# Expert stage of a diffusion-trunk kernel: one stream of 1 MB weight halves in a fixed order on three engines

## Chip, cores and metric

The kernel runs on one core of a Trainium2 chip. The metric is the device time of one launch in microseconds. The kernel before takes 2043.71 us (median of 3 runs, 2041.2 to 2043.97).

## What is computed

One layer of a trunk over 1024 latent tokens of width 1024 with a context prefix of 256: a token mixer, then an expert-choice SwiGLU mixture of 16 experts, then a final RMSNorm. The change concerns the mixture. Each expert takes the 128 tokens with the highest affinity for it:

```python
def expert_choice_ffn(h, w_router, w_gate, w_up, w_down):
    cap = EC_CAPACITY * n // N_EXPERTS                      # 128
    aff = softmax(h @ w_router, axis=-1)
    g, idx = lax.top_k(swapaxes(aff, 1, 2), cap)
    xg = h[bidx, idx]
    hid = silu(xg @ w_gate[e]) * (xg @ w_up[e])             # D_FF = 2816
    y = (hid @ w_down[e]) * g[..., None]
    return zeros_like(h).at[bidx, idx].add(y)
```

All is float32. The 16 experts have 16 x 3 x 1024 x 2816 weights, 554 MB, and each is read once.

## The kernel before

The mixer (the prologue) takes the first 435 us; the change leaves it alone. The rest, `moe`, is the expert stage.

Tiles. The hidden width 2816 of an expert is cut into six pieces j: five of 512 columns and one of 256. For each piece there is a gate-and-up unit and a down unit. A gate block or an up block of a 512 piece is 2 MB (128 partitions x 4096 words); the gate and up blocks of the 256 piece share one 2 MB array (`wt`); a down block is 2 MB, the last one 1 MB (`wdt`). An expert thus has 33 halves of 1 MB (128 x 2048 words), loaded in 17 transfers.

Splitting. TensorE (PE) is fed with a product of three: each float32 operand is split into a high and a low part (`split`, lines 226 to 232). ScalarE (ACT) copies the half to `hi` (line 227), VectorE (DVE) subtracts to get `lo` (line 228). `mm3` (line 611) issues hi*hi, hi*lo, lo*hi, so a half of 2048 columns costs 12 matmuls of 512 columns, in the 256 piece 24 of 256. There are five `raw` buffers of 2 MB (`NRAW`) and four `hi`/`lo` pairs of one half each (`NHL`): the pair of half m is free for half m+4 once the matmuls of half m are done.

Loop. For each expert e and piece j: `gate_up` (loads, splits, 48 matmuls to PSUM tile `gu`, Silu on ACT at line 1567, product on DVE at 1568, four transposes on PE to `ht` at 1572, split to `hh` and `hl`), then `down` of the piece before (24 matmuls to `y`). Behind the last piece of an expert, `y` is scaled on DVE (1597) and scatter-added to DRAM by GpSimd (POOL, 1598).

Beside it: a search for each expert's threshold (15 rounds `topk_iter`, two after each unit from n=1 to n=8: two DVE operations, eight PE matmuls to `tc`, four DVE operations; then `topk_end`, on DVE and POOL). Experts 0 and 1 have their tokens ranked in the prologue; expert 2 is the first that needs the search. `prep(e+1)` builds a one-hot matrix `oh` on DVE, gets the token numbers (`px`, `idx`) and gates (`pg`) by matmuls, and starts the gather `xg` on POOL (1451); `prep_t(e+1)` transposes and splits the rows to `xgh` and `xgl`. `last` (1621 to 1669) is the final norm.

Order. A scheduler lays out each engine's stream: it takes the program's order as priority and moves instructions past each other by its own account of when they will be ready. A few instructions are pinned by hand (`pin`), and `issue_after` puts the side work behind one split. Each engine works its stream off in that order.

## Time and profile before

| | us |
|---|---|
| median of 3 runs | 2043.71 |
| the profiled execution's own time | 2039.89 |
| its span, first to last instruction | 2038.0 |
| PE busy | 1911.7 (94%) |
| DVE busy | 1740.3 (85%) |
| ACT busy | 1334.7 (65%) |
| POOL busy | 203.4 (10%) |
| HBM read | 622.98 MB |

Times are microseconds from the span's start. A busy PE is not PE at its peak: matmuls overlap, and one of 512 columns is recorded with 0.39 us while the next starts 0.227 us after it. So the starts are read here, not the busy share. "[1.35 <-DVE lo L228]" says that the engine was idle for 1.35 us ahead of the instruction and that the `lo` of line 228 on DVE ended that. The granted TensorE clock is 0.976 on average; 1.00 stands for 2.4 GHz and 0.50 for 1.2 GHz.

### The profile page before, as it was taken

What the parts mean: (1) busy time and instruction counts of PE and PEld (TensorE: products, weight loads), DVE (VectorE), ACT (ScalarE), POOL (GpSimd) and SP (SyncE); (2) the same over time, 40 slices, a digit from 0 to 9 for tenths busy, and PEclk for the clock granted to TensorE, in tenths of its full rate; (3) what the DMA queues carried; (4) which work ended last, traced back from release to release, by engine and by line L of the source; (5) the groups of instructions that cost most, each with busy time, mean ns of one, the idle gap of its engine ahead of it and who ended that gap; (6) DMA issues with size and microseconds to landing.
All of it is one profiled execution on the core that took longest, in us unless ns stands there. A gap on an engine that the chain in (4) does not pass through costs nothing.

```text
span 2038.0 us, 23678 instructions
## 1 busy us (share of the span) xinstructions
PE 1911.7 (94%) x9434; PEld 1554.7 (76%) x9434; DVE 1740.3 (85%) x1641; ACT 1334.7 (65%) x1104; POOL 203.4 (10%) x141
## 2 busy tenths in 40 slices
PE   7989989959998999999999999999999999999994
PEld 2777778848887878787878787878787878778774
DVE  7888887799997888888888888888888898888886
ACT  6568643356775767676776676767667677676675
POOL 2311101130002000000010101010101010100011
PEclk9999989969999999999999999999999999999997
DMA  8444553579897989898999989898989898989994
GB/s 321 125 139 143 193 191 131 219 273 364 328 379 303 369 331 394 335 397 339 392 343 363 376 355 382 350 388 344 386 346 389 347 381 352 384 337 391 347 380 175
DMA packets 77517, 651.26 MB, mean 320 GB/s; under 512 B 8695, under 2 KB 16424, under 8 KB 42206
## 3 DMA queue, kind: packets, MB, share of 16 engines
q1 hardware_dynamic: 64286, 602.54, 75.5%
q0 software_dynamic: 10816, 38.82, 6.5%
q10 hardware_dynamic: 2304, 8.39, 1.0%
q8 instruction: 74, 1.21, 0.2%
q14 instruction: 37, 0.30, 0.0%
HBM read 622.98 MB, written 26.74 MB: 319 GB/s over the span
## 4 chain that ended last, share of the span: by engine, by line
PE 73%; DVE 12%; DMA 6%; issue 5%; ACT 3%; POOL 1%; SPq 0%; POOLq 0%; DVEq 0%; ACTq 0%
PE gu L611 43%; PE y L611 21%; DVE lo L228 5%; DMA mraw<-in_wmod_dram 3%; PE mx L611 3%; ACT hi L227 2%; PE ht L1572 2%; DVE macc L839 1%; DMA wm<-in_wmod_dram 1%; DVE ys L1597 1%; DMA trr<-in_trig_dram 1%; PE pq L611 1%; DVE g L716 1%; DMA x<-in_x_dram 1%; DMA accx<-xr 1%
## 5 line engine op out<-in xcount | busy, mean ns | idle before, releaser
L228 DVE TENSOR_TENSOR lo<-raw,hi 128x2048 fp32r<-128x2048 f32 (+1 forms) x531 | 1183.1, 2270 | 114.4 <-ACT hi L227 112.5
L227 ACT ACTIVATE hi<-raw 128x2048 fp32r<-128x2048 f32 (+1 forms) x531 | 981.2, 1894 | 85.1 <-PE gu L611 72.1
L611 PE MATMUL gu<-lo,xgh 128*128 128x512 f32 (+1 forms) x1536 | 579.7, 377 | 34.5 <-DVE lo L228 34.5
L611 PE MATMUL gu<-hi,xgh 128*128 128x512 f32 (+1 forms) x1536 | 575.7, 375 | 1.8 <-ACT xgh L227 1.6
L611 PE MATMUL gu<-hi,xgl 128*128 128x512 f32 (+1 forms) x1536 | 573.4, 373 | 1.7 <-DVE xgl L228 1.7
L611 PEld LDWEIGHTS gu<-lo,xgh 128*128 128x128 f32 x1536 | 290.1, 189 | 98.4 <-DVE lo L228 49.9
L611 PEld LDWEIGHTS gu<-hi,xgh 128*128 128x128 f32 x1536 | 290.2, 189 | 53.4 <-ACT xgh L227 2.1
L611 PEld LDWEIGHTS gu<-hi,xgl 128*128 128x128 f32 x1536 | 290.2, 189 | 51.6 <-DVE xgl L228 2.9
L611 PE MATMUL y<-hi,hl 128*128 128x512 f32 x704 | 280.6, 399 | 0.0
L611 PE MATMUL y<-lo,hh 128*128 128x512 f32 x704 | 279.0, 396 | 0.0
L611 PE MATMUL y<-hi,hh 128*128 128x512 f32 x704 | 275.7, 392 | 0.0
L1567 ACT ACTIVATE hid<-gu 128x512 f32<-128x512 f32 x96 | 54.0, 563 | 296.2 <-PE gu L611 296.2
L1598 POOL DMA_INDIRECT accx<-ys,idx x15 | 50.7, 3379 | 1125.6 <-DVE ys L1597 1051.0
L611 PEld LDWEIGHTS y<-lo,hh 128*128 128x128 f32 x704 | 132.6, 188 | 26.6
L611 PEld LDWEIGHTS y<-hi,hh 128*128 128x128 f32 x704 | 132.8, 189 | 25.5
L611 PEld LDWEIGHTS y<-hi,hl 128*128 128x128 f32 x704 | 132.9, 189 | 24.7
L227 ACT ACTIVATE hh<-ht 128x512 fp32r<-128x512 f32 x96 | 53.8, 561 | 88.9 <-PE ht L1572 88.9
L1568 DVE TENSOR_TENSOR hid<-hid,gu 128x512 f32<-128x512 f32 x96 | 61.5, 640 | 50.5 <-ACT hid L1567 49.4
L228 DVE TENSOR_TENSOR hl<-ht,hh 128x512 fp32r<-128x512 f32 x96 | 61.4, 640 | 4.3 <-ACT hh L227 4.3
L1451 POOL DMA_INDIRECT xg<-hxd,idx x16 | 42.3, 2642 | 210.6 <-DVE idx L1440 161.0
L1572 PE MATMUL ht<-k_ident,hid 128*128 128x128 f32 x352 | 54.7, 274 | 2.0 <-DVE hid L1568 2.0
L839 DVE SCALAR_TENSOR_TENSOR macc<-mraw,cond,macc 128x512 f32<-128x512 f32 x56 | 41.8, 748 | 16.1 <-DMA mraw<-in_wmod_dram 15.3
(425 smaller groups left out, 1862.4 us busy)
## 6 DMA issues: line engine op xcount, KB each, us to landing
raw<-in_wg_dram SPq DMA_DIRECT2D x80, 2048.0 KB, 9.8
raw<-in_wu_dram SPq DMA_DIRECT2D x80, 2048.0 KB, 10.6
raw<-in_wd_dram SPq DMA_DIRECT2D x78, 2048.0 KB, 9.7
raw<-in_wt_dram SPq DMA_DIRECT2D x15, 2048.0 KB, 10.0
mraw<-in_wmod_dram POOLq DMA_DIRECT2D x32, 512.0 KB, 4.6
raw<-in_wdt_dram SPq DMA_DIRECT2D x16, 1024.0 KB, 7.9
wm<-in_wmod_dram SPq DMA_DIRECT2D x16, 512.0 KB, 9.8
wr<-in_win_dram SPq DMA_DIRECT2D x24, 256.0 KB, 3.5
```

Source lines behind the costliest of these rows:

```text
L227: i = self.nc.scalar.activation(hi, src, AF.Copy)
L228: j = (eng or self.nc.vector).tensor_tensor(lo, src, hi, op=ALU.subtract)
L611: i = nc.tensor.matmul(out, l, r, start=st, stop=sp)
L716: V.tensor_tensor_scan(g[:, s], a[:, s], r[:, s], 0.0, op0=ALU.mult, op1=ALU.add)
L839: nc.vector.scalar_tensor_tensor(acc, w[:, i], c, acc, op0=ALU.mult, op1=ALU.add)
L1451: nc.gpsimd.indirect_dma_start(out=xg, out_offset=None, in_=self.hxd, in_offset=bass.IndirectOffsetOnAxis(ap=idx[:, :1], axis=0))
L1567: nc.scalar.activation(hid[:, 0:w], p[:, 0, 0:w], AF.Silu)
L1568: nc.vector.tensor_tensor(hid[:, 0:w], hid[:, 0:w], p[:, 1, 0:w], op=ALU.mult)
L1572: nc.tensor.transpose(q[:, 128 * b:128 * b + 128], hid[:, 128 * b:128 * b + 128], self.ident)
L1597: nc.vector.scalar_tensor_tensor(ys, self.y, gate, self.g2b, op0=ALU.mult, op1=ALU.mult)
L1598: nc.gpsimd.indirect_dma_start(out=self.accx, out_offset=bass.IndirectOffsetOnAxis(ap=idx[:, :1], axis=0), in_=ys, in_offset=None, compute ...
```

## The change

The weights of the stage become one list `S` of 528 halves (33 per expert) in the order in which PE uses them. Every half is loaded by itself (10 `raw` buffers of 1 MB instead of five of 2 MB), split by itself and multiplied by itself. The loop runs over the list: matmuls of half m, Silu and product where it ends a unit, split of half m+4 (`cut`), load of half m+10, then what `plan` has put behind half m. PE, ACT and DVE work in exactly the order of the program (`manual_schedule`); POOL and the queue of loads (SP) are still laid out by the scheduler. The transposes of `hid` follow one half after the end of their unit. The search takes one round every three halves, with the comparison (`topk_a`) three halves ahead of its matmuls (`topk_p`). `px` and `pg` become one PSUM tile, issued together. The one-hot matrix of the next expert is built four halves after the start of its host's second unit (fourth for expert 1) and multiplied two halves after the start of the next unit; the gathered rows are transposed in the fifth unit (sixth for expert 1). The finer cutting of the last two units (`DL`, `DS`, `FROM`) goes. Numbers of halves, buffers of `hi`/`lo`, matmuls and bytes stay.

```diff
--- before.py
+++ after.py
-    def topk_iter(self, i):
+    def topk_a(self, i):
+        V = self.nc.vector
+        cand, ge = self.tk[:2]
...
+    def topk_p(self, i):
+        ge = self.tk[1]
+        self.pc = self.pt(f"tc{i}")[:, 0:3 * E]
         for b in range(8):
-            nc.tensor.matmul(pc, self.ones2, ge[:, b].rearrange("p e q -> p (e q)"), start=b == 0, stop=b == 7)
-        V.tensor_scalar(g3.rearrange("p e q -> p (e q)"), pc, CAP - 0.5, None, op0=ALU.is_ge)
+            self.nc.tensor.matmul(self.pc, self.ones2, ge[:, b].rearrange("p e q -> p (e q)"), start=b == 0, stop=b == 7)
+
+    def topk_b(self, i):
+        V, T = self.nc.vector, self.T
+        g3, s3, inc = self.tk[2:]
...
-    NRAW, NHL = 5, 4
-    DL, DS, FROM = 2048, 1024, 95
+    NRAW, NHL = 10, 4
...
+    def gather(self, e, idx):
+        xg = self.mo.tile([128, D], F32, tag="xg", name=f"xg{e}", bufs=1)
+        self.nc.gpsimd.indirect_dma_start(out=xg, out_offset=None, in_=self.hxd,
+                                          in_offset=bass.IndirectOffsetOnAxis(ap=idx[:, :1], axis=0))
+        self.xe[e] = xg, idx
     def prep(self, e):
...
+        oh = self.mo.tile([128, 8, 128], BF16, tag="oh", name=f"oh{e}", bufs=1)
+        idx = self.mo.tile([128, 1], I32, tag="idx", name=f"idx{e}", bufs=3)
         g = self.mo.tile([128, 1], F32, tag="gate", name=f"gate{e}", bufs=3)
-        self.gate_pick(self.pt(f"pg{e}"), self.oh, self.aux[:, :, e], g)
+        slot = self.slot[:, e] if e < NR else self.slT[:, :, e]
+        self.nc.vector.tensor_tensor(oh, self.iota[:, None, :].to_broadcast([128, 8, 128]),
+                                     slot[:, :, None].to_broadcast([128, 8, 128]), op=ALU.is_equal)
+        yield
+        p = self.pt(f"px{e}")
+        for b in range(8):
+            self.nc.tensor.matmul(p[:, 0:2], oh[:, b], self.tokb[:, b], start=b == 0, stop=b == 7)
+        for b in range(8):
+            self.nc.tensor.matmul(p[:, 2:5], oh[:, b], self.aux[:, b, e], start=b == 0, stop=b == 7)
+        with self.nc.allow_low_precision(reason="whole numbers below 2**24"):
+            self.nc.vector.tensor_reduce(idx, p[:, 0:2], axis=mybir.AxisListType.X, op=ALU.add)
+        self.nc.vector.tensor_reduce(g, p[:, 2:5], axis=mybir.AxisListType.X, op=ALU.add)
+        self.gather(e, idx)
...
+    def make_stream(self):
+        a = self.a
+        self.S, self.at, self.end = [], {}, {}
+
+        def gu(e, j):
+            self.at[e, j] = len(self.S)
+            if j < 5:
+                for g, n in ((0, "wg"), (1, "wu")):
+                    for h in range(2):
+                        self.S.append(("g", e, j, g, h, a[n][e, j][:, 2048 * h:2048 * h + 2048]))
+            else:
+                for g in range(2):
+                    self.S.append(("g", e, j, g, 0, a["wt"][e][:, 2048 * g:2048 * g + 2048]))
+            self.end[e, j] = len(self.S) - 1
+
+        def dn(e, j):
+            if j < 5:
+                for h in range(2):
+                    self.S.append(("d", e, j, 0, h, a["wd"][e, j][:, 2048 * h:2048 * h + 2048]))
+            else:
+                self.S.append(("d", e, j, 0, 0, a["wdt"][e]))
+
+        prev = None
+        for e in range(E):
+            for j in range(6):
+                gu(e, j)
+                if prev is not None:
+                    dn(*prev)
+                prev = e, j
+        dn(*prev)
...
+        self.raws, self.hls = {}, {}
+        for m in range(2):
+            self.hls[m] = self.hl_tile(m)
+        for m in range(8):
+            self.load(m)
+        for m in range(8, 10):
+            self.raws[m] = self.raw_tile(f"raw{m}")
+        self.n0 = 0
...
-        t = self.ma.tile([128, 4096], F32, tag=f"raw{self.nr % self.NRAW}", name=name, bufs=1)
+        t = self.ma.tile([128, 2048], F32, tag=f"raw{self.nr % self.NRAW}", name=name, bufs=1)
...
-    def unit_tiles(self, w):
...
-    def load_unit(self, src, w=4096, fine=False):
...
-    def gate_up(self, e, j):
...
+    def load(self, m):
+        M = len(self.S)
+        if m < M:
+            self.raws[m] = self.raw_tile(f"raw{m}")
+            self.nc.sync.dma_start(self.raws[m], self.S[m][5])
+        elif m < M + 4:
+            t = 2 * (m - M)
+            src = self.accx.rearrange("(t p) c -> p t c", p=128)
+            self.fin.append(self.raw_tile(f"fin{t}"))
+            self.nc.sync.dma_start(self.fin[-1].rearrange("p (t c) -> p t c", t=2), src[:, t:t + 2])
+
+    def cut(self, m, pin=False):
+        if m >= len(self.S):
+            return
+        self.hls[m] = self.hl_tile(m)
+        self.split(self.raws.pop(m), *self.hls[m], pin=pin)
+
+    def half(self, m):
+        _, e, j, g, h, _ = self.S[m]
+        hi, lo = self.hls.pop(m)
+        if self.S[m][0] == "g":
+            xh, xl = self.xe[e][:2]
+            if g + h == 0:
+                self.gu[e, j] = self.pm.tile([128, 2, 512], F32, tag="gu", name=f"gu{e}{j}", bufs=2)
+            p = self.gu[e, j]
+            w = 512 if j < 5 else 256
+            nk = 2048 // w
+            for i in range(nk):
+                k, s = nk * h + i, slice(w * i, w * i + w)
+                self.mm3(p[:, g, 0:w], xh[:, k], xl[:, k], hi[:, s], lo[:, s], k == 0, k == KD - 1)
         else:
...
+            if j + h == 0:
+                self.y = self.pm.tile([128, D], F32, tag="y", name=f"y{e}", bufs=1)
+            hh, hl = self.hid[e, j]
+            for i in range(2):
+                b = 2 * h + i
+                for n in range(2):
+                    s = slice(1024 * i + 512 * n, 1024 * i + 512 * n + 512)
+                    self.mm3(self.y[:, 512 * n:512 * n + 512], hh[:, 128 * b:128 * b + 128],
+                             hl[:, 128 * b:128 * b + 128], hi[:, s], lo[:, s], j == 0 and b == 0, j == 5 and i == 1)
+
+    def act(self, e, j):
+        nc = self.nc
+        w, p = 512 if j < 5 else 256, self.gu.pop((e, j))
+        hid = self.hid[e, j] = self.mo.tile([128, 512], F32, tag="hid", name=f"hid{e}{j}", bufs=2)
         nc.scalar.activation(hid[:, 0:w], p[:, 0, 0:w], AF.Silu)
         nc.vector.tensor_tensor(hid[:, 0:w], hid[:, 0:w], p[:, 1, 0:w], op=ALU.mult)
+    def hid_t(self, e, j):
+        w, hid = 512 if j < 5 else 256, self.hid[e, j]
         q = self.pt(f"ht{e}{j}")
-        for b in range(nb):
-            nc.tensor.transpose(q[:, 128 * b:128 * b + 128], hid[:, 128 * b:128 * b + 128], self.ident)
+        for c in range(0, w, 128):
+            self.nc.tensor.transpose(q[:, c:c + 128], hid[:, c:c + 128], self.ident)
...
-    def down(self, e, j, h):
...
-    def last_loads(self):
...
+    def scatter(self, e):
+        _, _, idx = self.xe.pop(e)
+        ys = self.mo.tile([128, D], F32, tag="ys", name=f"ys{e}", bufs=2)
+        self.nc.vector.scalar_tensor_tensor(ys, self.y, self.xg_.pop(e), self.g2b, op0=ALU.mult, op1=ALU.mult)
+        self.nc.gpsimd.indirect_dma_start(out=self.accx, out_offset=bass.IndirectOffsetOnAxis(ap=idx[:, :1], axis=0),
+                                          in_=ys, in_offset=None, compute_op=ALU.add)
...
+    def plan(self):
+        post = {}
+
+        def at(m, f, *args):
+            post.setdefault(m, []).append(lambda: f(*args))
+
+        def steps(ms, gen):
+            for m in ms:
+                at(m, lambda: next(gen, None))
+
+        s = self.at
+        at(1, self.g2_load)
+        at(1, self.topk_start)
+        at(2, self.topk_a, 0)
+        at(3, self.gates)
+        for e in range(E):
+            for j in range(6):
+                at(self.end[e, j] + 1, self.hid_t, e, j)
+            if e + 1 < E:
+                j = 3 if e == 1 else 1
+                steps((s[e, j] + 4, s[e, j + 1] + 2), self.prep(e + 1))
+                m = s[e, 5 if e == 1 else 4]
+                steps((m, m + 1) if e == 1 else (m, m + 2), self.prep_t(e + 1))
+                at(self.end[e + 1, 0] + 1, self.scatter, e)
+        for i in range(15):
+            m = 5 + 3 * i
+            at(m, self.topk_p, i)
+            at(m, self.topk_b, i)
+            if i < 14:
+                at(m, self.topk_a, i + 1)
+        tail = self.topk_end()
+        steps((m, m + 3, m + 3, m + 4), tail)
+        at(m + 4, lambda: next(tail, None))
         for h in range(2):
+            at(s[0, 5] + 3 * h, self.g2_row, h)
+        at(s[E - 1, 1] + 2, self.last_prep)
+        return post
     def moe(self):
...
+            ET = mybir.EngineType
+            st.enter_context(tc.manual_schedule(engines={ET.PE, ET.Activation, ET.DVE}))
...
-            prev = None
-            for e in range(E):
-                for j in range(6):
-                    h = self.gate_up(e, j)
-                    if prev is not None:
-                        self.down(*prev)
-                    prev = (e, j, h)
-                    with tc.issue_after(last.ins):
-                        self.extra(e, j)
-                    if j == (5 if e == 1 else 4) and e + 1 < E:
-                        self.prep_t(e + 1)
-                    if e == E - 1 and j == 1:
-                        self.last_prep()
-            self.down(*prev)
+            post = self.plan()
+            M = len(self.S)
+            for m in range(M):
+                self.half(m)
+                if m in self.end.values():
+                    self.act(*self.S[m][1:3])
+                self.cut(m + 4)
+                self.load(m + 10)
+                for f in post.pop(m, ()):
+                    f()
             self.last()
```

## Rows read from the trace of the kernel before

**Rows 1.** Windows over the expert stage; columns: each engine's busy time, clock, DMA.
```profile
434.93:638.96 204.03, 197.96 (x1048) 160.65 (x1047) 192.52 (x212) 142.27 (x98) 18.14 (x11) 0.98 0.89 341
638.96:1909.88 1270.92, 1238.88 (x6058) 1022.35 (x6059) 1092.09 (x663) 878.09 (x611) 80.23 (x26) 1.00 0.93 364
1909.88:2010.74 100.86, 96.50 (x454) 79.48 (x453) 84.44 (x57) 70.17 (x59) 9.73 (x3) 1.00 0.86 331
2010.74:2038.03 27.29, 0.39 (x2) 0.00 (x0) 15.35 (x28) 10.15 (x19) 9.80 (x4) 0.56 0.43 173
```

**Rows 2.** Waits, 440 to 2000 us: who waited for whom; total, times, longest.
```profile
ACT hid L1567 <- PE gu L611: 293.2, 94, 5.8
```

**Rows 3.** Chain that ended last; columns: start, length, what.
```profile
737.46 10.89 PE gu L611 x48
...
1910.05 10.89 PE gu L611 x48
...
1944.10 2.30 DVE lo L228
```

**Rows 4.** Timeline of PE around the second gate-up unit of expert 7.
```profile
1142.31 0.40 PE L611 MATMUL gu<-hi,xgh 128*128 128x512 f32 x1
1144.07 0.50 PE L611 MATMUL gu<-lo,xgh 128*128 128x512 f32 x1 [1.35 <-DVE lo L228]
...
1156.14 0.39 PE L611 MATMUL y<-hi,hh 128*128 128x512 f32 x1
```

**Rows 5.** Timeline of ACT over the same stretch.
```profile
1126.16 7.32 ACT L227 ACTIVATE hi<-raw 128x2048 fp32r<-128x2048 f32 x4
1139.28 0.60 ACT L1567 ACTIVATE hid<-gu 128x512 f32<-128x512 f32 x1 [5.80 <-PE gu L611]
```

**Rows 6.** Timeline of DVE over the same stretch.
```profile
1141.72 2.29 DVE L228 TENSOR_TENSOR lo<-raw,hi 128x2048 fp32r<-128x2048 f32 x1 [1.12 <-ACT hi L227]
...
1145.72 11.09 DVE L228 TENSOR_TENSOR lo<-raw,hi 128x2048 fp32r<-128x2048 f32 x5
```

**Rows 7.** Timeline of ACT in expert 2, where no PE wait follows.
```profile
653.78 0.60 ACT L1567 ACTIVATE hid<-gu 128x512 f32<-128x512 f32 x1 [0.80 <-PE gu L611]
...
659.69 1.92 ACT L227 ACTIVATE hi<-raw 128x2048 fp32r<-128x2048 f32 x1 [0.58 <-PE gu L611]
```

**Rows 8.** Timeline of DVE in the same stretch of expert 2.
```profile
655.22 0.68 DVE L1568 TENSOR_TENSOR hid<-hid,gu 128x512 f32<-128x512 f32 x1
```

**Rows 9.** Timeline of PE in the same stretch of expert 2.
```profile
656.07 0.60 PE L1572 MATMUL ht<-k_ident,hid 128*128 128x128 f32 x4
```

**Rows 10.** Timeline of PE in experts 0 and 1: its waits.
```profile
452.60 0.66 PE L1572 MATMUL ht<-k_ident,hid 128*128 128x128 f32 x4 [1.99 <-DVE hid L1568]
...
619.77 0.35 PE L1438 MATMUL px<-tokb,oh 128*128 128x2 bf16 x8 [2.45 <-DVE oh L1435]
...
641.40 0.53 PE L611 MATMUL gu<-hi,xgl 128*128 128x512 f32 x1 [1.71 <-DVE xgl L228]
```

**Rows 11.** Windows right behind one of these waits, columns as in Rows 1.
```profile
621.25:624.67 3.42, 3.42 (x10) 2.65 (x10) 3.42 (x3) 0.60 (x1) 2.41 (x1) 0.50 0.34 77
```

**Rows 12.** Timeline of DVE: first step of one selection round, and what follows the round.
```profile
539.51 0.21 DVE L1387 TENSOR_SCALAR g<-tc 128x48 f32<-128x48 f32 x1 [0.47 <-PE tc L1386]
...
541.13 2.28 DVE L228 TENSOR_TENSOR lo<-raw,hi 128x2048 fp32r<-128x2048 f32 x1
```

**Rows 13.** Instructions on tile xg: time of the gathers from issue to landing.
```profile
DMA to landing us min/median/max: 5.5/12.5/13.9
```

**Rows 14.** DMA issues: KB each, median us from issue to landing.
```profile
raw<-in_wg_dram SPq DMA_DIRECT2D x80, 2048.0 KB, 9.8
...
raw<-in_wdt_dram SPq DMA_DIRECT2D x16, 1024.0 KB, 7.9
```

**Rows 15.** Windows of one expert, columns as in Rows 1: 85 us with the weight queue filled.
```profile
1128.20:1213.20 85.00, 82.68 (x386) 67.24 (x385) 73.39 (x43) 58.16 (x39) 6.17 (x2) 1.00 0.98 383
```

**Rows 16.** Chain that ended last, its end.
```profile
2005.30 1.28 ACT L1665
```

More of the change, by code (lines that the diff above doesn't have):

```diff
@@ L1479, in prep_t @@
         lo = self.mo.tile([128, KD, 128], F32R, tag="xgl", name=f"xgl{e}", bufs=2)
+        self.xe[e] = (hi, lo, idx)
         for g in range(2):
@@ L1530, in hl_tile @@
         return [pool.tile([128, 2048], F32R, tag=f"{t}{i}", name=f"{t}{name}", bufs=1) for t in ("hi", "lo")]
-    def unit_tiles(self, w):
-        out = [self.hl_tile(f"{self.nu}_{h}") for h in range(w // 2048)]
-        self.nu += 1
-        return out, self.ahead.pop(0) if self.ahead else None
-    def load_unit(self, src, w=4096, fine=False):
-        out, raw = self.unit_tiles(w)
-        if raw is None:
-            raw = self.raw_tile(f"raw{self.nu}")
-            n = self.DL if fine else w
-            for c in range(0, w, n):
-                self.nc.sync.dma_start(raw[:, c:c + n], src[:, c:c + n])
-        n = self.DS if fine else 2048
-        for h, (hi, lo) in enumerate(out):
-            for c in range(0, 2048, n):
-                self.split(raw[:, 2048 * h + c:2048 * h + c + n], hi[:, c:c + n], lo[:, c:c + n])
-        return out
@@ L1709, in moe @@
             self.pm = st.enter_context(tc.tile_pool(name="psM", bufs=1, space=bass.MemoryType.PSUM, reuse_waits="tile"))
-            self.xe, self.xg_ = {}, {0: self.gate0}
+            self.xe, self.xg_, self.fin, self.gu, self.hid = {}, {0: self.gate0}, [], {}, {}
             with tc.high_priority(offset=400):
-                self.prep(0)
+                self.gather(0, self.idx0)
             self.hold(1)
+            mo = self.mo
+            mo.tile([128, KD, 128], F32R, tag="xgh", name="z_xgh", bufs=2)
+            mo.tile([128, KD, 128], F32R, tag="xgl", name="z_xgl", bufs=2)
+            for t in ("hi", "lo"):
+                mo.tile([128, 2048], F32R, tag=f"{t}3", name=f"z_{t}3", bufs=1)
+            for t, dt in (("hid", F32), ("hh", F32R), ("hl", F32R)):
+                mo.tile([128, 512], dt, tag=t, name=f"z_{t}", bufs=2)
             A, G, V = self.pinned(nc.scalar), self.pinned(nc.gpsimd), self.pinned(nc.vector)
+            ET = mybir.EngineType
+            st.enter_context(tc.manual_schedule(engines={ET.PE, ET.Activation, ET.DVE}))
             self.unit0(A, G)
-            wu, raw = self.unit_tiles(4096)
-            self.split(raw[:, :2048], *wu[0], pin=True)
-            self.prep_t(0, pin=True)
-            last = self.split(raw[:, 2048:], *wu[1], pin=True)
-            self.first.append(wu)
+            self.cut(2)
+            for _ in self.prep_t(0):
+                pass
+            self.cut(3)
             self.accg = self.mo.tile([128, 2, 512], F32, tag="ys", name="accg2", bufs=2)
```

129 lines of the change are left out of this document (23 added, 106 removed).

## Prediction

> **What bounds the kernel now.** Read first the windows over the expert stage [rows 1]: experts 0 and 1 take 204.0 us, experts 2 to 14 take 1270.9 us (97.8 each), expert 15 takes 100.9, the tail behind PE's last matmul 27.3. The middle stage is two thirds of the time. DVE is busy 1092 of 1271 us there (86%), ACT 69%, the DMA engines 93%, so none of the three is full. PE is the bound, and the question is where it stands still.
>
> The chain of waits [rows 3] shows a fixed period: the first unit of expert 3 starts at 737.46 and that of expert 15 at 1910.05, twelve experts in 1172.6 us, 97.72 each. The timeline of PE shows where it stops [rows 4]: the second gate-up unit of expert 7 starts at 1142.31 and its 48 matmuls end at 1156.14, that is 13.83 us; an undisturbed unit takes 10.89 [rows 3]. The 2.94 us more are waits for `lo`; the first stands in the row.
>
> Why `lo` is late is on ACT [rows 5]. It has split four halves in a row by 1133.48 and then stands idle for 5.80 us, because the Silu of the running unit is next in its stream and that unit ends at 1139.1. The split of the next half, whose buffer was free long before (its last user, the first half of the unit that begins with the window of [rows 15] at 1128.2, had ended near 1131), comes behind the Silu. So DVE gets its `lo` at 1141.72 and the next at 1145.72 [rows 6], too late for 1142.31. Neither engine is short of time: the order of the stream costs it. Over the stage ACT waits 293.2 us for a unit's end [rows 2]; that costs nothing except at this place.
>
> The opposite order stands in the same trace: in expert 2, ACT splits each half just when its buffer comes free (idle 0.58 us ahead of it) [rows 7], the product starts at 655.22, 1.44 us behind the Silu at 653.78, and ends at 655.90 [rows 8], and the transposes start at 656.07 with no wait [rows 9].
>
> **The change, part by part.** All against the profiled execution: 2039.89 us, span 2038.0.
>
> *Order of the splits.* The split of half m+4 stands directly behind the matmuls of half m. A half is 12 matmuls, 10.89/4 = 2.72 us. Split m+4 begins about 0.2 us behind half m, takes 1.92 on ACT [rows 7] and 11.09/5 = 2.22 on DVE [rows 6]: ready 4.4 us behind half m, needed 3 x 2.72 = 8.2 us behind it. The 3.8 us of slack must cover whatever DVE does besides; the longest such group, behind a unit's end, is product, `hl` and `ys` (0.6 + 0.6 + 1.2), and DVE regains 2.72 - 2.22 = 0.5 us per half. So the 2.94 us go: 12 x 2.94 = 35.3 for experts 3 to 14 and 2.9 for expert 15. Expert 2 takes 98.5 from 638.96 to 737.46 and would take 97.72 - 2.94 = 94.8: 3.7. Expert 15 has one more wait where a `lo` of 2.30 us stands on the chain [rows 3]: 2.2. Sum: 44.1 us. Next late would be the weights, or the product that the transposes need (rivals 1 and 2).
>
> *Transposes one half behind their unit.* They are issued 12 matmuls, 2.72 us, behind the end of the unit, about 2.5 behind the start of the Silu. By rows 7 and 8 the product is ready 655.90 - 653.78 = 2.1 behind it, with a `lo` ahead of it on DVE, as in the new order. Margin 0.4 us; PE's stream, 2.72 us per half, queues behind it if it is late. I set this at 0, with up to 0.25 us for each of 84 transposes (21 us) in the range.
>
> *Threshold search in experts 0 and 1.* The same 15 rounds, 541.13 - 539.51 = 1.62 us of DVE each [rows 12], now one every three halves instead of two per unit, which is the same density. Six halves cost DVE 6 x 2.22 + 2 x 1.62 + 1.3 (product, `hl`) = 17.9 us, PE 6 x 2.72 + about 1.1 = 17.4. DVE is busy 192.5 of 204.0 us there [rows 1] and stays the bound: 0, between -2 and +4. The wait of 1.99 us at 452.60 [rows 10] stays too: the Silu's table load and the DVE work ahead of the product are the same.
>
> *Expert 2's selection.* Before, PE's `px` waited 2.45 us for `oh` [rows 10], which waits for POOL. Then the clock of PE fell to 1.2 GHz for 3.42 us [rows 11], which costs half of that, 1.7. Now `px` stands four halves behind `oh`, so both go: -4.1. But the gather now starts late. `idx` follows the split of that half on DVE, 4.4 us behind the half's end, the gather 0.4 later, and it lands 12.5 us on [rows 13]: 17.3. PE comes to the transposes of `xg` after four halves, one set of transposes and `px`: 3 x 2.72 + 2.9 + 0.9 = 12.0. It waits 5.3 us, and the clock falls again: +7.0. The bounds are the shortest and the longest landing, 5.5 and 13.9: no wait at all, or 6.7 + 1.7. I take the median, since the weight queue is full in both. The wait of 1.71 for `xgl` [rows 10] falls into expert 2, counted above. Another 1 us I allow for DVE's backlog ahead of `idx`. Sum for experts 0 and 1: about +4.
>
> *One stream of loads.* 33 transfers per expert instead of 17; on SP each still waits for the DVE subtraction that frees its buffer, only sooner, since 1 MB is freed at a time. Bytes and buffer space are the same. PE asks for the weights 3% faster. Before, the DMA engines moved 383 GB/s over 85 us with a share of 0.98 [rows 15]. An expert moves 364 GB/s x 97.8 us = 35.6 MB; at 383 that takes 93.0 us, below 94.8. So hidden, by 1.8 us. What a transfer of 1 MB costs more than half of one of 2 MB the trace doesn't show: a 1 MB load lands in 7.9 us, a 2 MB load in 9.8 [rows 14], but several are in flight. From below it is 0 (more, smaller loads may also fill the pocket between two buffers), from above (2 x 7.9 - 9.8)/2 = 3.0 us per added load if nothing overlapped; I take 0, since the 85 us at 0.98 hold loads of both sizes.
>
> The Trainium skill, in "DMA: Bandwidth & Descriptors", section "Measured (HBM→SBUF, 128 partitions, SWDGE, issued from GpSimd)", gives 341 GB/s for a 1 MB transfer and 425 for 16 MB. By its figure an expert would take 35.6 MB / 341 = 104 us, an estimate from that page, and the kernel about 2140 us. The trace's 383 GB/s with loads of 2 MB does not decide it.
>
> *Tail.* The last transposes now follow 12 matmuls instead of 7, and no finer cutting shortens them. ACT begins the norm's table load at 2005.30 [rows 16], 5.4 us ahead of PE's end at 2010.74 [rows 1]; now it begins about 4.4 ahead. The 27.3 us behind PE's end hang on ACT and DVE: +1.0, between 0 and +1.2.
>
> *Sum.* 2039.9 - 44.1 + 4.0 + 1.0 = 2000.8 us for an execution like the profiled one. That one is 3.8 us faster than the median of the runs shown, so against the median 2043.7 I forecast 2043.7 - 39.1 = 2004.6, call it 2004.
>
> **Rivals.**
>
> 1. *The weights become the bound.* Place: SP's queue between load m+10 and split m+10. It decides from the point where 16 more transfers per expert cost more than 94.8 - 93.0 = 1.8 us, 0.11 us each; from 97.7 - 93.0 = 4.7 us, 0.29 each, the kernel is slower than before. At 0.2 each an expert takes 96.2, +20 us on 14 experts: 2024. At 0.6 each it takes 102.6: 14 x 4.9 = 69 slower in the stage, 2113. For: the DMA share is 0.93 to 0.98 [rows 1, 15]. Against: deeper prefetch in smaller steps, and no wait of ACT for a load in the stage before. Chance 0.19, of which 0.05 for slower. The Trainium skill's rule above is this rival.
>
> 2. *The fixed order binds PE to DVE.* Six times per expert PE's stream stops at the transposes if the product is more than 0.4 us later than by rows 8. At 0.25 us each: 84 x 0.25 = 21, 2025; from 0.5 us each the gain is gone. Against: rows 9 show the tighter distance without a wait. Chance 0.12, of which 0.02 for slower.
>
> 3. *The change does not do what it says*: the waits come from the odd half (`wdt`) and the short 256 piece, where DVE must catch up, and they stay under any order. Then 2043.7 + 5 - a few = about 2045. Against: ACT's 5.80 us of idleness with a free buffer [rows 5]. Chance 0.06.
>
> **How the numbers follow.** Forecast with its own bounds (gather in time -7, small waits elsewhere that also go -4; search +4, gather +3, tail): 1993 to 2013, chance 0.63. Rival 1 gives 2013 to 2035 with 0.14, rival 2 2013 to 2035 with 0.10. A range of 1993 to 2027 holds about 8 in 10. A difference of 0.2%, 4.1 us, is about what a measurement can tell from no change. Faster: 0.63 + 0.14 + 0.10 = 0.87. Same: 0.05 (most of rival 3). Slower: 0.05 + 0.02 + 0.01 = 0.08.
>
> **What would show it.** Right: the second gate-up unit of an expert takes 10.9 us like the others, the period is 94.5 to 95, ACT is idle a little before each split instead of 5.8 us before one Silu. One PE wait of some 5 us stands ahead of expert 2's `xt`. Wrong: waits of ACT's `hi` for a load of `raw` (rival 1), waits ahead of `ht` on PE for `hid` (rival 2), or a `gu` unit that still waits for `lo` once per expert (rival 3). Experts 0 and 1 much shorter than 204 us would mean that DVE was not their bound.

## The result and the profile after

The changed kernel takes 1996.15 us (median of 4 runs, 1991.26 to 1996.76); beside it the kernel before took 2043.45 (4 runs, 2041.2 to 2043.97). The ratio is 0.9765, with a 95% interval of 0.9748 to 0.9783. The profiled execution took 1996.68 us, its span is 1994.9; against the profiled execution before that is 43.2 us less.

The windows of the changed kernel, cut at the same events as [rows 1] (columns as there): experts 0 and 1, experts 2 to 14, expert 15, the tail.

```profile
439.44:646.42 206.98, 198.27 (x1047) 161.44 (x1047) 191.94 (x210) 140.38 (x97) 17.47 (x13) 0.98 0.93 341
646.42:1871.55 1225.13, 1225.13 (x6059) 1024.50 (x6058) 1109.53 (x664) 905.88 (x611) 33.45 (x26) 1.00 0.99 379
1871.55:1966.79 95.24, 95.24 (x454) 79.77 (x453) 81.97 (x51) 69.72 (x51) 6.32 (x3) 1.00 0.81 316
1966.79:1994.90 28.11, 0.39 (x2) 0.00 (x0) 16.07 (x29) 10.95 (x21) 9.80 (x4) 0.55 0.42 168
```

Beside [rows 1]: the first stretch begins 4.5 us later and is 3.0 longer; experts 2 to 15 take 1320.4 us, not 1371.8, 51.4 less; the tail is 0.8 longer. 4.5 + 3.0 - 51.4 + 0.8 = -43.1. In the long stretch PE is now busy for all of it.

The chain that ended last (start, length, what) shows expert 3, expert 7 with its second unit, and expert 15. It answers to [rows 3]:

```profile
740.82 10.88 PE gu L611 x48
...
1117.82 10.88 PE gu L611 x48
1131.87 10.91 PE gu L611 x48
...
1871.71 10.88 PE gu L611 x48
```

The period is (1871.71 - 740.82) / 12 = 94.24 us, before 97.72. The second unit of expert 7, 13.83 us in [rows 4], is as short as any other.

ACT around the end of expert 7's first unit, and DVE beside it, answer to [rows 5] and [rows 6]:

```profile
1126.02 1.92 ACT L227 ACTIVATE hi<-raw 128x2048 fp32r<-128x2048 f32 x1 [0.80 <-PE gu L611]
1128.74 0.60 ACT L1618 ACTIVATE hid<-gu 128x512 f32<-128x512 f32 x1 [0.80 <-PE gu L611]
1129.23 1.91 ACT L227 ACTIVATE hi<-raw 128x2048 fp32r<-128x2048 f32 x1
```

```profile
1127.97 2.29 DVE L228 TENSOR_TENSOR lo<-raw,hi 128x2048 fp32r<-128x2048 f32 x1 [0.43 <-ACT hi L227]
1130.18 0.68 DVE L1619 TENSOR_TENSOR hid<-hid,gu 128x512 f32<-128x512 f32 x1
```

The 5.80 us of idleness ahead of one Silu have become at most 0.80 ahead of a split, and none ahead of the one behind the Silu: ACT takes each half when PE has freed its place. The waits of PE from 435 us to its end (total, times, longest) are only these:

```profile
PE ht L1625 <- DVE hid L1619: 8.3, 8, 2.0
PE rw L1228 <- DVE M L155: 5.5, 1, 5.5
PE xt L1497 <- DVE cnt L155: 0.4, 1, 0.4
PE xt L1497 <- DMA xg<-hxd,idx: 0.4, 1, 0.4
```

The first and the last lie in experts 0 and 1; `rw` is the start of the stage, below.

### The profile page after: what moved, and what is told of

It is laid out like the page before. It is cut to its first block, busy times and chain, and to the rows that moved or that the text cites. A ratio compares the mean times of both kernels' runs of the same rounds, so it can differ in the third digit from the quotient of the medians.

```text
span 1994.9 us, 24533 instructions
## 1 busy us (share of the span) xinstructions
PE 1895.8 (95%) x9434; PEld 1557.1 (78%) x9434; DVE 1754.8 (88%) x1636; ACT 1360.8 (68%) x1099; POOL 152.6 (8%) x141
## 4 chain that ended last, share of the span: by engine, by line
PE 78%; DVE 9%; issue 6%; DMA 5%; ACT 1%; POOL 1%; SPq 0%; POOLq 0%; DVEq 0%; ACTq 0%
PE gu L611 45%; PE y L611 22%; PE mx L611 4%; DMA mraw<-in_wmod_dram 3%; DVE lo L228 2%; PE ht L1625 2%; DMA wm<-in_wmod_dram 1%; DVE macc L839 1%; PE xt L1497 1%; DMA trr<-in_trig_dram 1%; PE hp L1181 1%; PE pq L611 1%; ACT hi L227 1%; DVE g L716 0%; DVE r L714 0%
## 5 line engine op out<-in xcount | busy, mean ns | idle before, releaser
L228 DVE TENSOR_TENSOR lo<-raw,hi 128x2048 fp32r<-128x2048 f32 x526 | 1200.9, 2297 | 134.5 <-ACT hi L227 132.2
L227 ACT ACTIVATE hi<-raw 128x2048 fp32r<-128x2048 f32 x526 | 1008.6, 1918 | 318.6 <-PE gu L611 207.7
L611 PE MATMUL gu<-lo,xgh 128*128 128x512 f32 (+1 forms) x1536 | 570.9, 372 | 0.0
L611 PE MATMUL y<-hi,hh 128*128 128x512 f32 x704 | 283.4, 403 | 0.0
L611 PE MATMUL y<-hi,hl 128*128 128x512 f32 x704 | 276.3, 392 | 0.0
L1635 POOL DMA_INDIRECT accx<-ys,idx x15 | 23.8, 1588 | 1007.0 <-DVE ys L1634 1007.0
L1625 PEld LDWEIGHTS ht<-k_ident,hid 128*128 128x128 f32 x352 | 43.8, 140 | 23.2 <-DVE hid L1619 11.7
```

Of the source, the lines that this page charges most:

```text
L227: i = self.nc.scalar.activation(hi, src, AF.Copy)
L228: j = (eng or self.nc.vector).tensor_tensor(lo, src, hi, op=ALU.subtract)
L611: i = nc.tensor.matmul(out, l, r, start=st, stop=sp)
L1625: self.nc.tensor.transpose(q[:, c:c + 128], hid[:, c:c + 128], self.ident)
L1635: self.nc.gpsimd.indirect_dma_start(out=self.accx, out_offset=bass.IndirectOffsetOnAxis(ap=idx[:, :1], axis=0), in_=ys, in_offset=None, co ...
```

## Experiments

Each is an edit of the changed kernel. Theory: the order of the splits makes the gain. Rivals: the smaller loads and buffers make it; or loads, DVE and the odd half hold the stage, so that an order could not.

### Loads of 2 MB again

```diff
-    NRAW, NHL = 10, 4          # raw tiles of 128x2048
+    NRAW, NHL = 5, 4           # raw tiles of 128x4096, two halves each
...
+            elif self.second(m):
+                self.nc.sync.dma_start(self.raw_half, full)
```

> The changed kernel with one thing undone: the weights come again in 2 MB transfers into five buffers of 2 MB (17 loads per expert), the order of splits, matmuls and transposes stays that of the stream. Theory (the order carries the gain, the loads were hidden before and after): the period of an expert stays at 94.2 to 94.7 us and the time at 1995 to 2002 us. Rival A (the gain came from buffers that come free 1 MB at a time, so that loads are never late): ACT waits for loads, the period goes back towards 97.7 us and the time to 2025 to 2045. Rival B (33 transfers of 1 MB cost more than 17 of 2 MB and hold the stage up a little): this kernel is faster than the changed one by 2 us or more.

1992.29 us (4 runs); ratio to the kernel before, run beside it, 0.9754 (0.9738 to 0.977), where the change had 0.9765 (0.9748 to 0.9783). Twelve experts take 1130.90 us in both kernels. The windows (columns as in [rows 1]), first with loads of 2 MB, then with loads of 1 MB in the changed kernel:

```profile
736.40:1867.30 1130.90, 1130.90 (x5594) 946.04 (x5593) 1024.17 (x613) 836.15 (x564) 30.83 (x24) 1.00 0.96 379
```

```profile
737.69:1868.59 1130.90, 1130.90 (x5594) 945.69 (x5593) 1024.20 (x613) 836.19 (x564) 30.85 (x24) 1.00 0.99 379
```

The 1 MB loads bring nothing that can be measured, and cost nothing. The median is 3.9 us below that of the changed kernel, more than the 2 us that rival B asks for; but the periods are equal to 0.01 us, and the intervals of the ratios overlap. The DMA share differs, 0.96 and 0.99, at the same 379 GB/s.

### Two splits late, once per expert

```diff
+                e, j = self.S[m][1:3]
+                late = self.at[e, 0] if e > 2 and self.S[m][0] == "g" and j == 0 else None
+                if late is None or m not in (late + 1, late + 2):
+                    if late is not None and m == late + 3:   # behind act(e, 0)
+                        self.cut(late + 5)
+                        self.cut(late + 6)
+                    self.cut(m + 4)
-                self.cut(m + 4)
```

> The changed kernel with one thing undone, once in each of experts 3 to 15: the splits of the second and the third half behind the expert's first unit are issued behind that unit's Silu and product, as before, and not one and two halves earlier. Everything else stays, the 1 MB loads too. Theory (the order carries the gain): the split then starts 0.6 us behind the unit's end and its low part is ready 0.6 (Silu) + 1.9 + 2.2 + 0.3 = 5.0 us behind it, while PE wants it after one half and the transposes of nothing else, 2.7 us: PE waits about 2.3 to 2.9 us per expert, 13 times, +30 to +38 us: 2026 to 2034 us; the period is 96.6 to 97.2. Rival A (smaller loads and buffers carry the gain): PE catches up, under +5 us, at most 2001.

One split comes two halves late, the next one half late. 2055.13 us (4 runs), ratio 1.0066 (1.0048 to 1.0084): 0.7% slower than before the change. The period is 99.00 us, 4.76 more. ACT, DVE and PE in expert 7 show the old picture again, and then a second wait:

```profile
1144.11 0.60 ACT L1618 ACTIVATE hid<-gu 128x512 f32<-128x512 f32 x1 [6.24 <-PE gu L611]
1144.61 7.31 ACT L227 ACTIVATE hi<-raw 128x2048 fp32r<-128x2048 f32 x4
```

```profile
1157.15 6.69 DVE L228 TENSOR_TENSOR lo<-raw,hi 128x2048 fp32r<-128x2048 f32 x3
1163.76 0.68 DVE L1619 TENSOR_TENSOR hid<-hid,gu 128x512 f32<-128x512 f32 x1
```

```profile
1148.89 0.50 PE L611 MATMUL gu<-lo,xgh 128*128 128x512 f32 x1 [1.42 <-DVE lo L228]
...
1164.49 0.88 PE L1625 MATMUL ht<-k_ident,hid 128*128 128x128 f32 x4 [1.93 <-DVE hid L1619]
```

The first wait is the one of [rows 4], 1.42 us where it was 1.35, and the unit takes 1.7 us longer. Then DVE, late, is in the second of three `lo` when the unit ends at 1159.68, and the product stands behind the third, so it comes late and PE stops again at the transposes, 2.1 us. In 7 of the 12 periods the granted clock then falls to 0.50 for some 3 us, and the period is 1.6 us longer (99.7 us instead of 98.1). 1.7 + 2.1 + 7/12 x 1.6 = 4.7. The theory holds and its price was too low: what was expected ended with the first wait. Of the rival nothing is left.

### Every split one half late

```diff
-                self.cut(m + 4)
+                self.cut(m + 3)        # from half 65 on
```

> The changed kernel with one size changed from half 65 on: the split of half m+3, not m+4, stands behind half m, so the slack of a split is 2 x 2.72 - 4.4 = 1.0 us and not 3.8. The prediction said that the slack must cover what DVE and ACT do besides: Silu and product behind a unit's end (0.6 + 0.7), the parts hh and hl behind its transposes (0.6 + 0.7), once per expert ys (1.3). Theory: PE waits 0.3 to 1.0 us at each of 6 units per expert, 14 experts, 25 to 85 us in all: 2021 to 2081, and the product comes late for the transposes in places. Rival (the distance does not matter as long as the order is right): under 10 us.

1994.57 us (1 run). PE waits nowhere from expert 2 on, and twelve experts take 1130.89 us. I expected 25 to 85 us; the rival was right. Yet ACT stands idle ahead of each Silu:

```profile
1126.62 0.60 ACT L1624 ACTIVATE hid<-gu 128x512 f32<-128x512 f32 x1 [3.52 <-PE gu L611]
1127.11 3.71 ACT L227 ACTIVATE hi<-raw 128x2048 fp32r<-128x2048 f32 x2
```

The split behind the Silu is one half late, its `lo` is ready at 1131.3, and PE wants it at 1132.2, two halves and a set of transposes behind the unit's end. So 1.0 us of slack (3.8 less one half) is enough, though by little: behind `ys` the third `lo` ends at 1137.5, and PE takes it at 1138.0. Idleness of ACT ahead of a Silu is no sign by itself; a second half late (as above) is what costs.

### No fixed order

```diff
-            st.enter_context(tc.manual_schedule(engines={ET.PE, ET.Activation, ET.DVE}))
```

> The changed kernel without the fixed order: the same stream, loads and distances, but PE, ACT and DVE are ordered by the scheduler from its own estimate of the durations. Theory (what counts is that a split stands ahead of a Silu that waits for a unit's end): if the scheduler still puts a Silu ahead of a split that could run, the units behind it wait again and the time is 2015 to 2045; if it keeps the stream's order, 1990 to 2002. Rival (the order of the program text, not the fixing, makes the gain): 1990 to 2002 with the same order on ACT.

2018.87 us (1 run), period 96.41. The scheduler packs five splits and leaves one for behind the Silu:

```profile
1118.47 9.18 ACT L227 ACTIVATE hi<-raw 128x2048 fp32r<-128x2048 f32 x5
1131.16 0.60 ACT L1618 ACTIVATE hid<-gu 128x512 f32<-128x512 f32 x1 [3.52 <-PE gu L611]
```

PE loses 0.3 to 1.1 us in several units. So the stream, the loads and the program's order alone bring about half of the gain (23.9 us of time, but only 1.31 of the 3.48 us of the period), the fixing the rest. One run stands behind this split.

### How fast the weights can come

Both kernels leave out the third matmul of each product of the stage, so that PE no longer bounds it; one has loads of 1 MB, the other of 2 MB.

```diff
-                self.mm3(p[:, g, 0:w], xh[:, k], xl[:, k], hi[:, s], lo[:, s], ...)
+                self.mm2(p[:, g, 0:w], xh[:, k], xl[:, k], hi[:, s], lo[:, s], ...)   # without xl*hi
```

> Left out: of the three matmuls of each product in the expert stage the third one (high part of the weight with the low part of the activation), so PE has a third less to do there; loads, splits and everything else stay as in the changed kernel, with 1 MB transfers. It measures how fast the weights can come when PE does not hold them back. PE then needs about 33 x 1.8 + 2.5 = 62 us per expert, ACT about 33 x 1.92 + 5 = 68, DVE 33 x 2.22 + 8 = 81. Theory (the loads are hidden, but by little): the DMA engines take over as the bound, the period is 88 to 94 us, DMA share 0.99, and ACT waits for loads. If 379 GB/s was already their limit, the period is 94.0 to 94.3 as in the changed kernel and the next gain from PE would be nothing. If they have room, DVE bounds at 81 to 84 us.

> As the light kernel with 1 MB transfers (the same third of the matmuls of the expert stage left out), but with 17 transfers of 2 MB per expert instead of 33 of 1 MB. The difference of the two periods over 16 transfers is the price of one more transfer. Theory (hidden and nearly free): the two periods agree within 0.8 us, 0.05 us per added transfer. Rival (a transfer of 1 MB costs 0.11 us or more above half of one of 2 MB): this period is shorter by 1.8 us or more. The opposite (small loads fill the pocket between two buffers): this period is longer.

1871.1 us with 1 MB, 1858.39 us with 2 MB (1 run each). Twelve experts, first with 1 MB, then with 2 MB:

```profile
726.46:1748.92 1022.46, 844.22 (x3912) 678.80 (x3912) 1000.61 (x613) 824.49 (x565) 30.84 (x24) 0.94 1.02 415
```

```profile
721.35:1738.96 1017.61, 841.48 (x3912) 676.99 (x3913) 999.35 (x613) 820.79 (x565) 30.83 (x24) 0.94 1.01 420
```

The periods are 85.20 and 84.80 us: 0.40 over 16 transfers is 0.025 us for each added one. That is 4.9 of the 12.7 us between the two runs; another 5.1 lie ahead of these windows, 4.1 of them already ahead of the first `px`, in the prologue, which is the same. I had expected the DMA engines to take over as the bound, at 88 to 94 us. DVE is busy 98% of both windows, so the loads need not even be the bound, and what a transfer costs where they are, no run shows: they can bring at least 415 GB/s, 9.0 us per expert faster than the changed kernel asks. My step with a room of 1.8 us took the 383 GB/s of [rows 15] for a limit because the share beside it was 0.98.

### The search without its distance

```diff
-            if i < 14:
-                at(m, self.topk_a, i + 1)
+            at(m, self.topk_a, i)      # ahead of topk_p(i)
```

> The changed kernel with the second part of the change undone: each round's compare on DVE is issued directly ahead of its matmuls, not three halves ahead. The compare then stands behind the low part of half m+4, ready about 0.2 + 1.9 + 2.2 + 0.8 = 5.1 us behind half m, while PE wants it at once. Theory (the distance hides this): PE waits 4 to 5 us in each of 15 rounds, partly with the clock at 1.2 GHz behind it: +50 to +90 us, all of it in experts 0 and 1. Rival (DVE bounds the window, PE's waits are its slack): under 15 us.

2102.3 us (1 run). Waits of PE (total, times, longest):

```profile
PE tc L1388 <- DVE ge L1381: 79.7, 15, 6.3
```

That is 5.3 us for each round, with the granted clock at 0.84 over experts 0 and 1 (0.98 in the changed kernel): this stretch takes 311 us to its last transposes, 107 more, where I expected 50 to 90. It is the waits and the clock together; in a fixed order PE has nothing else to take meanwhile.

### Experts 0 and 1: where to let PE wait

```diff
-                at(self.end[e, j] + 1, self.hid_t, e, j)
+                at(self.end[e, j] + (2 if e < 2 else 1), self.hid_t, e, j)
```

> The changed kernel with one edit: in experts 0 and 1 the transposes of a unit's product are issued two halves behind the unit's end and not one. PE waits there 8.3 us for the product in eight places in the changed kernel, and twice the clock falls behind such a wait. Theory (rival 2's mechanism, in the search window alone: the product comes up to 2.4 us late because search rounds stand ahead of it on DVE, while DVE has 15 us of idle time in the 207): the waits go, experts 0 and 1 take 197 to 201 us instead of 207 and the time falls by 6 to 10 us. Rival (DVE is the bound of the window, as the prediction said, so a wait that goes comes back elsewhere, as waits for lo): under 3 us.

1992.33 us (4 runs), ratio 0.9756 (0.9739 to 0.9772). The waits at `ht` fall from 8.3 us to 0.7, but in their place stands

```profile
PE xt L1497 <- DMA xg<-hxd,idx: 5.0, 1, 5.0
PE y L611 <- DVE hl L228: 1.2, 1, 1.2
```

With two more of 0.9 us the waits of PE in these experts add up to 8.8 us, in the changed kernel to 8.7. From their first gate-up matmul to that of expert 2 it takes 205.65 us, in the changed kernel 206.98, in the kernel with 2 MB loads 204.65: no gain beyond the scatter, so the rival was right about the sum. (The last transposes of expert 1, at 205.5 and 204.0 us, are no common mark, since the edit itself puts them one half later.) Counted from the first gate-up matmul, PE comes to `px` 8.2 us earlier than in the changed kernel, but DVE to `idx` only 5.1 us: in this kernel `px` stands at 612.54, and

```profile
613.44 6.69 DVE L228 TENSOR_TENSOR lo<-raw,hi 128x2048 fp32r<-128x2048 f32 x3
620.04 0.15 DVE L1469 TENSOR_REDUCE idx<-px 128x1 int32<-128x2 f32 x1
```

The next kernel adds two edits to this one, whose diffs stand under the last two experiments: `idx` ahead of the split of its half, and the earlier start.

> The changed kernel with three edits: the later transposes in experts 0 and 1, the earlier start, and the second step of a selection (px, idx, gate, gather) issued ahead of the split of that half, so that idx no longer stands behind a low part on DVE. With the later transposes alone PE came to px 8 us earlier, but idx followed px by 8 us of DVE backlog and the gathered rows came 5.3 us late, so nothing was won. Theory (the backlog of DVE, not its total work, stops PE, and only at idx): idx follows px within 3 us, the 5.3 us wait and the clock's fall behind it go, expert 2's rows are there in time: from the first gate-up matmul to the last transposes of expert 1 (204.0 us in the changed kernel, 205.5 with the later transposes) 195 to 200 us, and with the 2.2 us of the start 1984 to 1990 us. Rival (DVE is the bound of the window in total, 192 us of work in 207): the gain stays at the 2 to 4 us of the single edits, 1990 to 1994, with new waits for lo behind expert 1.

1990.65 us (5 runs), ratio 0.9755 (0.9741 to 0.9768), 204.95 us to the first gate-up matmul of expert 2. The forecast of 195 to 200 us failed: PE waits the 5.0 us as before. `idx` stands ahead of that half's `lo`, but `lo` of two earlier halves (4.48 us) are still ahead of it, so it follows `px` by 5.3 us and not by 7.5. Those 2.2 us are lost again at the gather, which now has the `lo` behind `idx` beside it:

```profile
617.33 2.92 POOL L1451 DMA_INDIRECT xg<-hxd,idx  x1 [8.81 <-DVE gate L1470]
```

With later transposes alone this instruction took 1.06 us and the rows landed 9.2 us behind its start, here 11.4. As `idx` did not come within the 3 us that the theory asks, the run does not decide whether the backlog at `idx` alone stops PE. That left the question whether DVE's total work is the bound.

```diff
         for i in range(15):
             m = 5 + 3 * i
+            if i >= 12:
+                continue
...
```

> Left out: the last 3 of the 15 rounds of the threshold search, so the thresholds of experts 2 to 14 lack their last six bits; everything else is the changed kernel, the rest of the selection at its old places. It takes 3 x 1.62 = 4.9 us of work from DVE and 0.5 us from PE in expert 1. From the first gate-up matmul to the last transposes of expert 1 the changed kernel and the variants with the same order take 201.2 to 204.0 us, 1.7 us of it for each fall of the clock; the later transposes moved PE's wait from the products to the gathered rows and left the sum at 204.8 to 205.5. Theory (DVE's total work bounds this stretch, and PE's waits are where it shows): the stretch shortens by 3.5 to 5 us, to 197 to 199 us, expert 1 from 103 to 98 to 99.5, and the time by as much. Rival (the waits come from the places in the order, not from DVE's work): it shortens by no more than PE's own 0.5 us to 1 us.

1992.58 us (4 runs), ratio 0.9753 (0.9736 to 0.9771). From the first gate-up matmul to the last transposes, which stand at their old place here, the stretch takes 199.7 us with one fall of the clock in it. Less the 1.7 us that a fall costs it is 198.0, against 200.6 for the changed kernel less its two falls, and 201.2 with `idx` first, in which there was none. That is 2.6 to 3.2 us, of which about 1 is PE's own, for 4.1 us less of busy DVE (189.0 and 184.9). Between theory and rival: 7.3 us of waits at `ht` stay, at the same places. DVE's total is only part of it; what would shorten these two experts stays open.

### The start of the stage

```diff
-            st.enter_context(tc.manual_schedule(...))
             self.unit0(A, G)
-            self.cut(2)
+            self.cut(2, pin=True)
...
+            st.enter_context(tc.manual_schedule(...))
```

> The changed kernel with one edit: the first unit's last piece, the splits of halves 2 and 3 and the transposes of expert 0's rows are issued ahead of the hand-ordered part, each engine's in program order, as the kernel before did. In the changed kernel the low part of half 2 (2.28 us) stands on DVE between the last two ranking steps, which PE waits for ahead of the transposes of xg. Theory: from the first matmul px to the first gate-up matmul the time falls from 11.2 us to 9.0, as before, and the run by about 2.2 us. Rival (the 2.28 us are only moved, since DVE is behind in expert 0 anyway): the start is earlier, but the end of expert 1 is not.

1990.03 us (4 runs), ratio 0.9739 (0.9723 to 0.9756). DVE and PE in the changed kernel, where the `lo` stands between two ranking steps:

```profile
433.43 2.28 DVE L228 TENSOR_TENSOR lo<-raw,hi 128x2048 fp32r<-128x2048 f32 x1
...
435.70 1.13 DVE L155 TENSOR_SCALAR_CACHE_REDUCE M<-R,lg 128x896 bf16<-128x896 f32 x1
```

```profile
436.90 0.34 PE L1228 MATMUL rw<-onesb,M 128*128 128x1 bf16 x7 [5.52 <-DVE M L155]
```

and PE with the edit:

```profile
434.25 0.35 PE L1228 MATMUL rw<-onesb,M 128*128 128x1 bf16 x7 [3.32 <-DVE M L155]
```

From the first `px` to the first gate-up matmul it takes 8.96 us, not 11.16, and the two experts behind it 204.0 to their last transposes, as in the changed kernel: 2.2 us, as the theory says. Its median is the lowest of the versions that compute the whole result; its interval still overlaps that of the changed kernel.

### The gather beside a subtraction

```diff
+                if m in self.early:        # second step of prep(e + 1)
+                    self.early[m]()
                 self.cut(m + 4)
```

> The changed kernel with one edit: the second step of a selection (px, idx, gate, gather) is issued ahead of the split of that half, in experts 0 to 13. In the changed kernel DVE stands idle or between instructions when GpSimd writes the gather's descriptors (1.0 us); before, a low part of 2.2 us followed idx directly and the same instruction took 2.8 to 3.0 us, the first packets 6.0 us behind its start and not 3.8. Theory (a DVE subtraction beside it slows GpSimd's descriptor work): the gather's instruction takes 2.5 to 3.1 us again and the first packets come 5.5 to 6.7 us behind its start; the time stays within 3 us of the changed kernel, since only expert 2 waits for its rows, 0.7 us. Rival (its length follows the loads in the queues, not DVE): it stays at 1.0 us.

1994.24 us (1 run). GpSimd and DVE in this kernel, for expert 2 and for expert 3:

```profile
624.15 2.95 POOL L1451 DMA_INDIRECT xg<-hxd,idx  x1 [8.21 <-DVE gate L1470]
...
685.09 0.99 POOL L1451 DMA_INDIRECT xg<-hxd,idx  x1 [19.98 <-DVE gate L1470]
```

```profile
623.87 2.29 DVE L228 TENSOR_TENSOR lo<-raw,hi 128x2048 fp32r<-128x2048 f32 x1
...
685.17 2.29 DVE L228 TENSOR_TENSOR lo<-raw,hi 128x2048 fp32r<-128x2048 f32 x1 [0.29 <-ACT hi L227]
```

Where the `lo` began 0.28 us ahead of the gather, the gather lasted until 0.94 us behind the end of the `lo` (626.16), and its first packets came 6.1 us behind its start. Where the gather began first, by 0.08 us, it took 0.99 us and its packets came after 4.3. The theory holds where a `lo` follows `idx` at once (experts 1 and 2), and the start decides, not the mere presence. The Trainium skill, "SBUF — State Buffer", section "SBUF: two separate sides", says that a DVE instruction with two inputs in SBUF and a GpSimd instruction that reads SBUF share a pair of ports, that the one that starts first has it for the whole instruction, and that the other is blocked. The gather's two lengths agree; the `lo` that began 0.08 us behind a gather took 2.29 us as always and shows no block.

## Why the prediction came out

The forecast was 2004 us, 39.1 less than before, with 1993 to 2013 for its own mechanism; the median is 1996.15. Between the two profiled executions it is 43.1 us of span. The 4.0 us more are in the main two errors of opposite sign, so the closeness is in part luck: the order of the splits gave 7.3 us more than forecast, and the start, which was left out, cost 4.5. The medians differ by 47.3, in the main since the profiled execution before was 3.8 us quicker than its median.

**Order of the splits: right, a little small.** Forecast 44.1 us for experts 2 to 15, measured 51.4. The mechanism is shown by the two late splits, which bring the wait of [rows 4] back as 1.42 us. The mis-sized term is the 2.94 us per expert: the period fell by 3.48. The unit of the sum did fall nearly as counted, from 13.83 to 10.99 us. Another 0.60 lies in the 256 piece, whose 48 matmuls took 6.35 us with transposes of `xg` in between and now take 5.75 without. The kernel before had a short wait for `lo` there, which I had not counted; the matmul ahead of it starts at 1216.85, so it costs some 0.4 us of the 0.60:

```profile
1217.32 0.38 PE L611 MATMUL gu<-lo,xgh 128*128 128x256 f32 x1 [0.19 <-DVE lo L228]
```

**Start: missed.** I set nothing. The stage began 4.5 us later. 2.2 of it are the `lo` between the ranking steps, shown by the edit that takes it back. The other 2.3 are there ahead of the stage already: the first `px`, of expert 0, stands at 428.28, before at 425.92, and in the other profiled executions, whose prologue is the same, between 424.7 and 431.6, so this is the scatter of executions.

**Experts 0 and 1: the sum near by luck, two of its terms wrong.** Forecast +4, measured +3.0; in the profiled executions of the kernels that leave these experts' order alone (2 MB loads, the late splits, the earlier start) the same stretch takes 204.65 to 206.95 us, +0.6 to +2.9. `px` no longer waits and the clock no longer falls behind it, as said. But the wait for the gathered rows was 0.4 us and not 5.3. `idx` and the gather follow `px` by 4.4 and 4.8 us, as counted, and PE comes to `xt` after 12.2; the term that was off is the landing time, for which I took the median of 12.5 [rows 13]. In the changed kernel it is, for this gather alone and then for all 16:

```profile
DMA to landing us min/median/max: 7.7/7.7/7.7
```

```profile
DMA to landing us min/median/max: 5.9/8.5/11.6
```

About 2 of the 4.8 us are GpSimd's part, 1.06 us here and 3.00 before, where a `lo` ran beside it. The rest is not traced to a cause: with 1.06 or 1.07 us this gather landed after 5.9 to 9.2 us in the other runs, with 2.9 to 3.0 after 10.3 to 11.9, and the slowest of the 16, that of expert 1, took 11.6 us with a GpSimd part of 1.01.

In place of that wait stand 8.3 us of waits at `ht` with two falls of the clock, 1.7 us each. That is rival 2, which I priced per transposition over all experts: it acts in eight places of the search stretch, where DVE has search steps and a backlog ahead of the product, and nowhere else. (The first of the eight, 1.94 us, goes with a `lo` that GpSimd held up; see the last section.) By [rows 9] the distance is enough, where no such work stands in between. With later transposes a wait of 5.0 us did appear, but not by the forecast's sum: there `idx` follows `px` by 7.5 us, and the rows land after 9.2. That DVE bounds these experts, as I said, is borne out only in part, by the kernel with 12 rounds.

**Loads: hidden, as said, with a wrong limit.** An added transfer cost the period 0.025 us where DVE was busy 98% of the time. My bound from above, 3.0, was that of one load of 1 MB; for an added load it is 2 x 7.9 - 9.8 = 6.0. The room is 9.0 us or more, not 1.8. So rival 1 deserved less than its 0.19. The estimate of 104 us per expert from the Trainium skill's 341 GB/s for a transfer of 1 MB ("DMA: Bandwidth & Descriptors", section "Measured (HBM→SBUF, 128 partitions, SWDGE, issued from GpSimd)") is refuted here for loads in a stream: 94.24 us at 379 GB/s, and 85.20 at 415 with the light kernel.

**Tail: right.** Forecast +1.0, measured +0.8: ACT begins the norm's table load 4.6 us ahead of PE's end, where I had said 4.4 and it was 5.4 before.

**Rival 3** (waits stay under any order) is refuted by the period and by a PE that waits nowhere from expert 2 on.

## What to carry to other kernels

Read the order of an engine's stream first where no engine is full: an instruction that waits for the end of a unit must not stand ahead of work whose data is ready by more than the slack allows. Here one half late was free, and two halves late (with the next split one half late) cost 4.8 us on average: 1.7 at once, 2.1 because the late engine passes its delay on to the next product, the rest by the clock. A fixed order takes away the scheduler's freedom, so every pair of a producer and a consumer on another engine needs its distance: three halves for the search were worth 107 us. Where PE waits for an engine with a backlog, moving the wait to another place won nothing here.

## What the runs showed of the hardware

- The share of DMA busy time is no measure of room: 0.96 and 0.99 at the same 379 GB/s with 2 MB and 1 MB loads, 0.98 at 383 [rows 15], and 1.02 at 415.
- The gather's instruction on GpSimd takes 0.99 us, or 2.95 when a DVE subtraction of 2.29 us began just ahead of it. The small GpSimd steps of the selection show the same: two of the same shape in the changed kernel are

```profile
610.56 0.43 POOL L1426 TENSOR_TENSOR sel<-sel,m 128x128 f32<-128x128 f32 x1 [0.41 <-DVE sel L1425]
...
611.36 2.48 POOL L1427 TENSOR_TENSOR sel<-sel,m 128x128 f32<-128x128 f32 x1
```

  and beside the second DVE had a `lo` from 611.19 on.
- The other way round it is the `lo` that is held up. In expert 0 of the changed kernel a GpSimd addition (in `g2_load`) and a `lo` are

```profile
448.09 4.22 POOL L1709 TENSOR_TENSOR accg<-accg,bg 1x1024 f32<-1x1024 f32 x1 [8.83 <-DMA bg<-in_rows_dram]
```

```profile
450.44 4.02 DVE L228 TENSOR_TENSOR lo<-raw,hi 128x2048 fp32r<-128x2048 f32 x1 [0.24 <-ACT hi L227]
```

  The `lo` takes 4.02 us and not 2.29, and ends 2.15 us behind the addition. The product stands behind it, and PE waits 1.94 us at `ht`, the first of the eight waits. Where the addition met the `lo` otherwise, with 2 MB loads and with the earlier start, this wait is 0.21 us.
- PE waits of some 2 us brought the granted clock down to 0.50 in some cases and not in others: of the three waits of 1.8 to 2.0 us at `ht` in the changed kernel two did, and of the twelve of 1.9 us in experts 3 to 14 of the kernel with two late splits seven.
